# Last tile's layer norm read from PSUM, an early GpSimd broadcast, and step lists in another order, in a two-layer hybrid encoder

## The chip, the cores and the metric

The kernel runs on one core of a Trainium2 chip. A core has five engines with an instruction queue each: TensorE (PE; its weight loads are shown as PEld), VectorE (DVE), ScalarE (ACT), GpSimd (POOL) and SyncE (SP), which here only issues DMAs. The metric is the device time of one execution in microseconds (us); several executions are timed and the median counts.

## The reference

The input x has 256 tokens of 1024 values. Two layers of three sublayers each follow, every one closed by a layer norm over the residual (ALPHA is the fourth root of 4):

```
x <- LN(ALPHA*x + 0.5*SwiGLU_1(x))
x <- LN(ALPHA*x + Mixer(x))      layer 0: bidirectional chunkwise mLSTM, layer 1: windowed attention
x <- LN(ALPHA*x + 0.5*SwiGLU_2(x))

swiglu(x)    = (silu(x @ w_g) * (x @ w_u)) @ w_out        hidden width 2816
LN(x)        = (x - mean) * rsqrt(var + 1e-5) * g + b     over the 1024 values of a token
mLSTM        4 heads; input and forget gates per direction; log-forget sums along the tokens,
             running maxima, weights exp(...), then (q k^T * weights) @ v, divided by a normaliser,
             a norm per head, times sigmoid(o), @ w_out
attention    16 query heads on 4 key/value heads, |t-s| <= 128, a linear distance bias, a sink
             logit per head, softmax, @ v, @ w_out
```

All data are float32, and so is the output.

## The kernel before, in words

**Products.** Every float32 operand is split in two reduced-precision parts: ACT casts the high part (`w_hi`, `xT_hi`, `h_hi`), DVE subtracts it from the original to get the low part (`w_lo`, ...). `mm3` (line 691) makes one product of three matmuls, hi x hi, hi x lo and lo x hi. So each 128x1024 word of weights costs a DMA, one ACT cast and one DVE subtraction before PE can use it.

**Stages.** The 256 tokens are two tiles of 128. Six stages run one after the other: ffn, mlstm, ffn, ffn, attn, ffn. In an ffn, most of the up projection goes through Strassen-Winograd blocks of 512 gate and 512 up columns: `strassen` (line 907) returns seven products named P1, P2, S1, S2, S3, S4 and A22, each in two halves, one word of weights each. Some words are sums of two blocks of weights: either DVE adds two loaded words, or a DMA of POOL's queue adds the second block onto the first in SBUF (`bring`, line 926). The mLSTM's value projection is one such block as well; there A22's words are completed by a `bring` in `fourth_word`.

**The order on PE is written by hand.** The strings at lines 47 to 57 name the steps of PE in order, with a count behind `*`. In the blocks of an ffn (FIRST, FULL, SHUT, OPEN): `d` is one chunk of the down projection (12 matmuls of 512 columns), `T0` and `T1` turn a block's hidden values of token tile 0 and 1 (four transposes into a PSUM bank, then a high and a low part by ACT and DVE), `a` and `b` are the side columns, `x1` to `x4` the sums of x that Strassen's products need, `p` what is left of the stage before. OPEN is the first block of a stage with five blocks, FIRST the first of the stage with four (the run's first), SHUT the last of a stage, FULL those between. `T1` turns the values of the block before; in them the product `e<-g,e` is made after A22. In MIXES (mLSTM): `u` is a unit of the output gate, `q` a unit of the query and key projection (three matmuls of 256 columns), `g` the gate projection with the scans behind it, `c` four small transposes that turn the scans' results into columns, `H0` to `H3` the score products of a head, `M0` to `M3` its mixing with the values, `sig` a sigmoid. In HEADS (attention): `P`, `S`, `E`, `N`, `T`, `V` are a head pair's score products, masked scores, exponentials, scaling, transposes and value products, `y0` and `y1` units of the output projection.

**The order on the other engines is planned.** `Book` (line 253) notes each step without running it. `cost` gives each a length, `latest` a due time (counted back from the PE step that needs it), and `sequence` walks through a simulated time: of the steps that could start first on an engine, the one with the earliest due time goes next. The same walk gives each tile its buffer and each result its PSUM bank; the bank that is free first is taken, and one that PE hasn't fully written goes ahead of a written one. `emit` (line 591) then issues every step, so that all instructions carry line 600 in the profile. On the chip each engine runs its queue in this order and waits where an input is late. For a plain transfer in POOL's queue the plan takes the landing from `FEW` (line 63); one such transfer is `most`, another the small loads (`few`).

**The mLSTM's scans** (line 1249) start when ACT has copied the gates' forget half from PSUM to `gl`. A chain of DVE and ACT steps follows; two small transfers of POOL's queue bring four rows of the result to partitions 0, 32, 64 and 96 of `most`, and `weights(h)` (line 1290) spreads one of these rows over all partitions for each head and direction with `partition_broadcast` on POOL; ACT takes exponentials, and POOL masks them (`affine_select`).

**The layer norm** is the class `Norm` (line 761). "Seeded" means that ACT writes ca*x into the output's PSUM bank before the matmuls, which then add onto it. In most cases ACT copies the finished half to x with its sum, squares it, and DVE applies the mean with the gain, then the scale with the bias. The power -1/2 is one instruction on POOL (`tensor_tensor` with `OP.pow`). In the last stage the second token tile is "parted": it isn't seeded; DVE adds ca*x and the PSUM result into SBUF and takes statistics there. `tail` (line 827) orders the last chunks. In the last stage it does the first three chunks of the second half of columns, then all chunks of the first half, and then the last three chunks of the second half in two quarters of 256 columns, each in a bank of its own, so that only a quarter's work stands behind the last matmul.

Of the kernel before, what the change touches and what calls it, by code (L numbers as in the profile page):

```python
# [15 lines left out]
OP = mybir.AluOpType  # L16
# [34 lines left out]
OWN = [(5, 0), (6, 0), (7, 0)]  # L51
MIXES = ('P1*2 u*4 P2*2 u*2 p u*2 x1 u*4 x3 g x2 u*4 x4 S1*2 S2*2 S4*2 S3*2 q*7 A22*2 q*1 c q*29 '
         'q*1 H0 q*2 H1 q*8 M0 q*16 sig u*2 H2 M1 u*1 H3 u*3 M2 u*2 M3 u*8')
FIRST = "P1*2 d T1 P2*2 S1*2 S2*2 d S3*2 S4*2 d A22*2 T0"
FULL = "P1*2 d T1 P2*2 S1*2 S2*2 d S3*2 S4*2 d A22*2 T0 d"
SHUT = "P1*2 d T1 P2*2 S1*2 S2*2 d*2 S3*2 S4*2 A22*2 T0"
OPEN = "a*1 P1*2 a*3 p P2*2 x1 b*1 x2 S1 b*1 S1 x3 x4 b*1 S2*2 b*1 S4*2 t S3*2 d A22*2 T0"
# [5 lines left out]
FEW = {"most": 6600.0, "few": 9500.0}  # L63
# [189 lines left out]
class Book:  # L253
# [79 lines left out]
    def cost(self, s):  # L333
# [3 lines left out]
        if s.engine == "PE":  # L337
# [5 lines left out]
            if narrow != self.narrow:  # L343
                s.takes, self.narrow = s.takes + (195.0 if narrow else 146.0), narrow
# [259 lines left out]
def trunk_kernel(ctx: ExitStack, tc: tile.TileContext, x, ffn_w_in, ffn_w_out, ln_g, ln_b, ml_w_in, ml_gate_b,  # L604
# [156 lines left out]
    class Norm:  # L761
        def __init__(self, t, ca, eps, last=False, seeded=True):
            self.t, self.ca, self.eps, self.last = t, ca, eps, last
            self.parted = last and t
            self.seeded = seeded and not self.parted
            if self.parted:
                self.stats = few[:, 171:189].rearrange("p (h s) -> p h s", h=3)
            else:
                self.sums = small("sums", [128, 6])
# [4 lines left out]
        def half(self, h, y):  # L774
            z = xt[self.t][:, h * 512:(h + 1) * 512]
            if self.seeded:
                nc.scalar.activation(z, y, AF.Copy, accum_out=self.sums[:, h:h + 1])
            elif self.parted:
                nc.vector.scalar_tensor_tensor(z, z, self.ca, y, op0=OP.mult, op1=OP.add)
                nc.vector.bn_stats(self.stats[:, h], z)  # L780
            else:
                nc.vector.scalar_tensor_tensor(z, z, self.ca, y, op0=OP.mult, op1=OP.add, accum_out=self.sums[:, h:h + 1])

        def first(self, h, y):
            z = xt[self.t][:, h * 512:(h + 1) * 512]
            nc.vector.scalar_tensor_tensor(z, z, self.ca, y, op0=OP.mult, op1=OP.add)

        def quarter(self, h, q, y):
            z = xt[self.t][:, h * 512 + q * 256:h * 512 + (q + 1) * 256]
            nc.vector.tensor_add(z, z, y)  # L790
            nc.vector.bn_stats(self.stats[:, h + q], z)

        def finish(self):
# [16 lines left out]
            for s_ in cuts:  # L810
                nc.vector.scalar_tensor_tensor(z[:, s_], z[:, s_], mean, self.gain[0][:, s_],
                                               op0=off, op1=OP.mult)
# [14 lines left out]
    def tail(y, h, todo, norm, last, turn_at, between=None):  # L827
# [16 lines left out]
        for j, (o, n) in enumerate(order):  # L844
# [5 lines left out]
            if last and j == half - 1:  # L850
                norm[1].first(1, y[1][1])
            if n == full - 1:
                norm[1].half(o, y[1][o])
        if last:
            for q in range(2):
                yq = bank((128, 256))
                for n in range(half, full):
                    c, get = todo[1][n]
                    mm3(yq, h(c, 1), pair(get(), A, 0, slice(512 + 256 * q, 768 + 256 * q)), n == half, n == full - 1)
                norm[1].quarter(1, q, yq)  # L860
# [328 lines left out]
    def mlstm(l, n, pending, last):  # L1189
# [59 lines left out]
        def scans():  # L1249
            nc.scalar.copy(gl, pg[64:128])  # L1250
            nc.vector.scalar_tensor_tensor(fa[r], pg[f_], gbias[f_], gl[f_], op0=OP.add, op1=OP.add)
# [379 lines left out]
```

## Time and profile before

| | |
|---|---|
| median of 3 runs (range) | 905.94 us (904.21 to 906.06) |
| the profiled execution's own time | 904.78 us |
| its span in the trace | 903.0 us |
| busy: PE, DVE, ACT, POOL | 99%, 91%, 73%, 19% |
| mean granted clock of TensorE | 0.998 |
| DMA | 244 GB/s mean, 220.07 MB |

A line of the profile shows start and length in us, engine, line, operation, output<-inputs by the program's names, shape, and in brackets how long the engine had been idle and which instruction ended that. Groups show a count, busy time and mean length in ns. Lengths of neighbouring instructions on one engine overlap a little, on PE by almost half, so spacing is read from starts. "Waits" lists who waited for whom: total, times, longest.

### The profile page before, as it was taken

To read this page: it belongs to the slowest core of one execution; us is meant where nothing else is said; L and a number is where in the kernel's file an instruction comes from. 1 tells how busy PE (TensorE), PEld (TensorE's weight loads), DVE (VectorE), ACT (ScalarE), POOL (GpSimd) and SP (SyncE) were. 2 spreads that over 40 slices of the span, in tenths; PEclk is the share of its full clock that TensorE was granted. 3 is DMA by queue.
4 is the path that set the end of the run, shared out by engine and by line. 5 is a ranking of instruction groups with operands and counts; after the bars stand their busy time and mean duration, and the time that the engine had idled before them with its cause. 6 is when DMAs were issued, how large, how long until landed. Compare 5 with 4: busy or idle time off the path is not lost.

```text
span 903.0 us, 12647 instructions
## 1 busy us (share of the span) xinstructions
PE 890.6 (99%) x4375; PEld 741.9 (82%) x4375; DVE 824.9 (91%) x1011; ACT 655.8 (73%) x923; POOL 168.4 (19%) x200
## 2 busy tenths in 40 slices
PE   9999999999999999999999999999999999999996
PEld 7888888888888888888888888888898788888785
DVE  7999998699997999999889999996889999999974
ACT  7777676687876887776669766776789888677651
POOL 0121221220521221112021211130133231211100
PEclk9999999999999999999999999999999999999999
DMA  9999998927486989999975999999542688999931
GB/s 318 378 306 271 275 314 266 293 78 230 161 299 175 229 243 324 292 265 279 362 192 164 241 296 314 290 251 374 166 125 95 181 191 230 319 274 267 291 85 46
DMA packets 107744, 220.07 MB, mean 244 GB/s; under 512 B 7288, under 2 KB 23696, under 8 KB 107680
## 3 DMA queue, kind: packets, MB, share of 16 engines
q1 hardware_dynamic: 84000, 174.09, 54.2%
q0 software_dynamic: 23680, 45.18, 29.0%
q8 instruction: 34, 0.56, 0.2%
q14 instruction: 30, 0.25, 0.1%
HBM read 218.18 MB, written 1.05 MB: 243 GB/s over the span
## 4 chain that ended last, share of the span: by engine, by line
PE 72%; DVE 15%; issue 6%; DMA 4%; ACT 2%; POOL 1%; DVEq 0%; POOLq 0%; ACTq 0%
PE pw L600 44%; PE py L600 28%; DVE w_lo L600 8%; DMA b<-in_ffn_w_in_dram 3%; DVE b L600 1%; ACT sc L600 1%; DVE e L600 1%; DMA raw<-in_ffn_w_in_dram 1%; DVE S L600 1%; DVE scan L600 1%; DVE x L600 1%; DVE pr L600 1%; DVE pv L600 0%; DVE xT_lo L600 0%; DVE sc L600 0%
## 5 line engine op out<-in xcount | busy, mean ns | idle before, releaser
L600 ACT CAST w_hi<-b 128x1024 fp32r<-128x1024 f32 x280 | 292.0, 1053 | 103.1 <-PE py L600 50.6
L600 DVE TENSOR_TENSOR w_lo<-b,w_hi 128x1024 fp32r<-128x1024 f32 x280 | 334.0, 1217 | 9.5 <-ACT w_hi L600 9.1
L600 PE MATMUL pw<-w_hi,S 128*128 128x512 f32 x640 | 205.7, 390 | 0.0
L600 POOL DMA_DIRECT2D b<-in_ffn_w_in_dram x80 | 97.1, 1217 | 501.0 <-DVE b L600 172.6
L600 DVE TENSOR_TENSOR w_lo<-raw,w_hi 128x1024 fp32r<-128x1024 f32 (+1 forms) x150 | 178.6, 1207 | 11.4 <-ACT w_hi L600 10.5
L600 ACT CAST w_hi<-raw 128x1024 fp32r<-128x1024 f32 (+1 forms) x150 | 155.1, 1041 | 37.1 <-PE pw L600 15.9
L600 PE MATMUL pw<-w_hi,xT_hi 128*128 128x512 f32 (+1 forms) x400 | 156.6, 393 | 1.4 <-DVE h_lo L600 0.8
L600 PE MATMUL pw<-w_hi,xT_lo 128*128 128x512 f32 (+1 forms) x400 | 154.5, 388 | 0.2 <-DVE xT_lo L600 0.2
L600 PE MATMUL pw<-w_lo,xT_hi 128*128 128x512 f32 (+1 forms) x400 | 153.3, 386 | 0.0
L600 PEld LDWEIGHTS pw<-w_hi,S 128*128 128x128 f32 x640 | 120.1, 188 | 26.1 <-DVE h_lo L600 1.1
L600 PE MATMUL py<-w_hi,h_hi 128*128 128x512 f32 x317 | 125.5, 396 | 0.0
L600 PE MATMUL pw<-w_lo,S 128*128 128x512 f32 x320 | 124.5, 389 | 0.0
L600 PE MATMUL py<-w_hi,h_lo 128*128 128x512 f32 x317 | 123.7, 390 | 0.0
L600 PE MATMUL py<-w_lo,h_hi 128*128 128x512 f32 x317 | 123.4, 389 | 0.0
L600 DVE TENSOR_TENSOR b<-b,b 128x1024 f32<-128x1024 f32 x74 | 90.1, 1218 | 0.9
L600 PEld LDWEIGHTS pw<-w_hi,xT_lo 128*128 128x128 f32 x400 | 75.1, 188 | 17.5 <-DVE xT_lo L600 2.2
L600 PEld LDWEIGHTS pw<-w_hi,xT_hi 128*128 128x128 f32 x400 | 75.0, 188 | 17.0 <-DVE h_lo L600 1.6
L600 PEld LDWEIGHTS pw<-w_lo,xT_hi 128*128 128x128 f32 x400 | 75.1, 188 | 13.9
L600 PEld LDWEIGHTS pw<-w_lo,S 128*128 128x128 f32 x320 | 60.1, 188 | 12.3
L600 PEld LDWEIGHTS py<-w_hi,h_lo 128*128 128x128 f32 x317 | 59.5, 188 | 12.7
L600 PEld LDWEIGHTS py<-w_lo,h_hi 128*128 128x128 f32 x317 | 59.6, 188 | 11.8
L600 PEld LDWEIGHTS py<-w_hi,h_hi 128*128 128x128 f32 x317 | 59.5, 188 | 11.6
(208 smaller groups left out, 1130.1 us busy)
## 6 DMA issues: line engine op xcount, KB each, us to landing
b<-in_ffn_w_in_dram SPq DMA_DIRECT2D x152, 512.0 KB, 8.1
raw<-in_ffn_w_out_dram SPq DMA_DIRECT2D x88, 512.0 KB, 8.3
b<-in_ffn_w_in_dram POOLq DMA_DIRECT2D x80, 512.0 KB, 9.0
raw<-in_ffn_w_in_dram SPq DMA_DIRECT2D x36, 256.0 KB, 7.0
raw<-in_ml_w_in_dram SPq DMA_DIRECT2D x16, 512.0 KB, 6.3
raw<-in_at_w_in_dram SPq DMA_DIRECT2D x12, 512.0 KB, 9.1
b<-in_ml_w_in_dram SPq DMA_DIRECT2D x8, 512.0 KB, 6.3
raw<-in_ml_w_out_dram SPq DMA_DIRECT2D x8, 512.0 KB, 3.5
```

Source lines behind the costliest of these rows:

```text
L600: getattr(engines[s.engine], s.name)(*[real(x) for x in s.args], **{k: real(x) for k, x in s.kw.items()})
```

## The change

1. `Norm`: the parted tile is seeded like the others, its statistics are taken by `bn_stats` straight from PSUM, and the first product of `finish` reads the PSUM pieces (kept in `held`) and writes x in SBUF. The DVE adds of `half`, `first` and `quarter` are gone.
2. `tail`: after the first three chunks of the second half, ACT copies the bank in two pieces of 256 columns into two new banks, and the quarters' matmuls add onto these copies instead of starting from zero.
3. `scans`: one `partition_broadcast` of a row of `gl` into `most` right after the copy of `gl`. Its result is overwritten by the two transfers.
4. The lists HEADS, MIXES, FIRST, FULL, SHUT and OPEN are in another order.
5. The plan's costs: the landing of `most` is 8500 ns instead of 6600, and a matmul that switches between 64 and 128 rows of the array costs 255 and 230 ns more instead of 195 and 146.

```diff
 HEADS = (...
-         'q*1 S5 T31 E5 y0*1 q*5 T40 V3 y0*1 P6 S6 E6 N6 T41 y0*1 N5 y0*1 V4 T50 P7 T51 S7 E7 y0*2 '
-         'N7 V5 y1*1 T60 T61 y0*2 y1*1 V6 T70 y1*1 T71 y1*2 V7 y0*1 y1*1 y0*3')
+         'S5 T31 y0*1 q*1 E5 q*5 T40 V3 y0*1 P6 S6 E6 N6 T41 y0*1 N5 y0*1 V4 T50 P7 T51 S7 E7 y0*2 '
+         'N7 V5 y1*1 T60 T61 y0*2 V6 y1*1 T70 y1*1 T71 y1*2 V7 y0*1 y1*1 y0*3')
...
-MIXES = ('P1*2 u*4 P2*2 u*2 p u*2 x1 u*4 x3 g x2 u*4 x4 S1*2 S2*2 S4*2 S3*2 q*7 A22*2 q*1 c q*29 '
-         'q*1 H0 q*2 H1 q*8 M0 q*16 sig u*2 H2 M1 u*1 H3 u*3 M2 u*2 M3 u*8')
-FIRST = "P1*2 d T1 P2*2 S1*2 S2*2 d S3*2 S4*2 d A22*2 T0"
-FULL = "P1*2 d T1 P2*2 S1*2 S2*2 d S3*2 S4*2 d A22*2 T0 d"
-SHUT = "P1*2 d T1 P2*2 S1*2 S2*2 d*2 S3*2 S4*2 A22*2 T0"
-OPEN = "a*1 P1*2 a*3 p P2*2 x1 b*1 x2 S1 b*1 S1 x3 x4 b*1 S2*2 b*1 S4*2 t S3*2 d A22*2 T0"
+MIXES = ('P1*2 u*4 P2*2 u*2 p u*2 x1 u*4 x3 g x2 u*4 x4 S1*2 S2*2 S4*2 S3*2 q*8 c q*5 A22*2 q*25 H0 '
+         'q*2 H1 q*8 M0 q*16 M1 sig u*2 H2 u*1 H3 u*3 M2 u*2 M3 u*8')
+FIRST = "T1 P1*2 d P2*2 S1*2 S2*2 S4 d*2 S3*2 S4 A22*2 T0"
+FULL = "P1*2 d T1 P2*2 S1*2 S2*2 d S3*2 S4*2 d A22*2 d T0"
+SHUT = "T1 P1*2 d P2*2 S1*2 S2*2 d*2 S3*2 S4*2 A22*2 T0"
+OPEN = "a*1 P1*2 a*3 p P2*2 x1 b*1 x2 S1 b*1 S1 S2 x3 x4 b*1 S2 b*1 S4*2 t S3*2 d A22*2 T0"
...
-FEW = {"most": 6600.0, "few": 9500.0}
+FEW = {"most": 8500.0, "few": 9500.0}
...
             if narrow != self.narrow:
-                s.takes, self.narrow = s.takes + (195.0 if narrow else 146.0), narrow
+                s.takes, self.narrow = s.takes + (255.0 if narrow else 230.0), narrow
...
             self.parted = last and t
-            self.seeded = seeded and not self.parted
+            self.seeded = seeded
+            self.held = []
...
         def half(self, h, y):
             z = xt[self.t][:, h * 512:(h + 1) * 512]
-            if self.seeded:
+            if self.parted:
+                nc.vector.bn_stats(self.stats[:, h], y)
+                self.held.append((slice(h * 512, h * 512 + 512), y))
+            elif self.seeded:
                 nc.scalar.activation(z, y, AF.Copy, accum_out=self.sums[:, h:h + 1])
-            elif self.parted:
-                nc.vector.scalar_tensor_tensor(z, z, self.ca, y, op0=OP.mult, op1=OP.add)
-                nc.vector.bn_stats(self.stats[:, h], z)
             else:
...
-        def first(self, h, y):
-            z = xt[self.t][:, h * 512:(h + 1) * 512]
-            nc.vector.scalar_tensor_tensor(z, z, self.ca, y, op0=OP.mult, op1=OP.add)
-
         def quarter(self, h, q, y):
-            z = xt[self.t][:, h * 512 + q * 256:h * 512 + (q + 1) * 256]
-            nc.vector.tensor_add(z, z, y)
-            nc.vector.bn_stats(self.stats[:, h + q], z)
+            nc.vector.bn_stats(self.stats[:, h + q], y)
+            self.held.append((slice(h * 512 + q * 256, h * 512 + q * 256 + 256), y))
...
             cuts = [slice(0, 512), slice(512, D)] if self.last else [A]
-            for s_ in cuts:
-                nc.vector.scalar_tensor_tensor(z[:, s_], z[:, s_], mean, self.gain[0][:, s_],
+            for s_, v in self.held or [(s_, z[:, s_]) for s_ in cuts]:
+                nc.vector.scalar_tensor_tensor(z[:, s_], v, mean, self.gain[0][:, s_],
                                                op0=off, op1=OP.mult)
...
             if last and j == half - 1:
-                norm[1].first(1, y[1][1])
+                yq = [bank((128, 256)) for _ in range(2)]
+                for q in range(2):
+                    nc.scalar.copy(yq[q], y[1][1][:, 256 * q:256 * q + 256])
...
             for q in range(2):
-                yq = bank((128, 256))
                 for n in range(half, full):
                     c, get = todo[1][n]
-                    mm3(yq, h(c, 1), pair(get(), A, 0, slice(512 + 256 * q, 768 + 256 * q)), n == half, n == full - 1)
-                norm[1].quarter(1, q, yq)
+                    mm3(yq[q], h(c, 1), pair(get(), A, 0, slice(512 + 256 * q, 768 + 256 * q)), False, n == full - 1, True)
+                norm[1].quarter(1, q, yq[q])
...
         def scans():
             nc.scalar.copy(gl, pg[64:128])
+            nc.gpsimd.partition_broadcast(most[:, 0], gl[0:1])
```

## The prediction

> **What bounds the kernel now.** I read the page first, then PE's waits over the whole run, then the order of time on PE, DVE and POOL at the places the change touches.
>
> ```profile
> span 903.0 us, 12647 instructions
> PE 890.6 (99%) x4375; PEld 741.9 (82%) x4375; DVE 824.9 (91%) x1011; ACT 655.8 (73%) x923; POOL 168.4 (19%) x200
> ...
> L600 ACT CAST w_hi<-b 128x1024 fp32r<-128x1024 f32 x280 | 292.0, 1053 | 103.1 <-PE py L600 50.6
> ```
>
> TensorE works for 99% of the span, and DVE, which subtracts out every low half after ACT has cast the high one, is close behind at 91%. The change removes no matmul, so it can win only what PE waits, and what stands behind the last matmul.
>
> ```profile
> PE pw L600 <- DVE h_lo L600: 0.8, 1, 0.8
> PE py L600 <- DVE a_lo L600: 0.7, 1, 0.7
> PE pw L600 <- DVE k_lo L600: 0.4, 2, 0.2
> ...
> PE py L600 <- DVE q_lo L600: 0.3, 1, 0.3
> ```
>
> These are the largest of PE's waits behind the start-up; none reaches a microsecond. The a_lo wait opens the mixing of the mLSTM's first head:
>
> ```profile
> 237.47 0.39 PE L600 MATMUL py<-v_hi,a_hi 128*128 128x258 f32 x1 [0.16 <-ACT a_hi L600]
> 237.69 0.28 PE L600 MATMUL py<-v_lo,a_hi 128*128 128x258 f32 x1
> 238.63 0.39 PE L600 MATMUL py<-v_hi,a_lo 128*128 128x258 f32 x1 [0.66 <-DVE a_lo L600]
> ```
>
> Printed waits leave out part of a gap, so I take it from the starts: 0.94 where 0.12 is usual (21 such matmuls, the seven q units, fill 214.39 to 216.91 in the rows below). With the 0.16 ahead of it that is 1.0 us. The h_lo wait is at a seam between two Strassen blocks of the last stage:
>
> ```profile
> 846.16 0.60 PE L600 MATMUL pw<-ident,e 128*128 128x128 f32 x4
> ...
> 849.14 0.39 PE L600 MATMUL py<-w_hi,h_lo 128*128 128x512 f32 x1
> 850.30 0.50 PE L600 MATMUL pw<-w_hi,xT_hi 128*128 128x512 f32 x1 [0.77 <-DVE h_lo L600]
> ```
>
> There are 1.16 us between two starts, against 0.23 (216.91 to 217.14 below): 0.9 us. P1 of the new block takes the bank that T0's transposes filled at 846.16, and it is free only when DVE has read it, behind another product:
>
> ```profile
> 848.96 0.68 DVE L600 TENSOR_TENSOR e<-g,e 128x512 f32<-128x512 f32 x1
> 849.56 0.68 DVE L600 TENSOR_TENSOR h_lo<-pw,h_hi 128x512 fp32r<-128x512 f32 x1
> ```
>
> **The change part by part.**
>
> *The early broadcast.* POOL in the mLSTM, the landing of the `most` transfers, the durations of the broadcasts, the input of the next power, and ACT's copy of the keys:
>
> ```profile
> 201.88 1.20 POOL L600 DMA_DIRECT2D b<-in_ml_w_in_dram  x1 [0.53 <-DVE w_lo L600]
> 219.62 1.21 POOL L600 DMA_DIRECT2D most<-scan  x2 [16.55 <-ACT w_hi L600]
> 227.59 4.21 POOL L600 PARTITION_BROADCAST wt<-most  x4 [6.76 <-ACT v_hi L600]
> ...
> 249.29 0.81 POOL L600 TENSOR_TENSOR hrs<-hrs,few 128x2 f32<-128x2 f32 x1 [6.91 <-DVE k_lo L600]
> ...
> DMA to landing us min/median/max: 1.7/1.7/1.7
> ...
> L600 POOL PARTITION_BROADCAST wt<-most x8: 547/548/2967, 227.6 to 241.8; - x8
> ...
> 246.36 0.17 DVE L600 TENSOR_SCALAR hrs<-hmv 128x2 f32<-128x2 f32 x1
> ...
> 230.90 0.58 ACT L600 ACTIVATE k_hi<-pw 128x512 fp32r<-128x512 f32 x1
> ```
>
> Both `most` transfers have been issued by 220.83 and land 1.7 after their issue, by about 222; the first broadcast starts at 227.59 and takes 2.97, where others take 0.55. The power at 249.29 likewise starts 2.8 after its input (246.36+0.17). Both gaps are 6.8 to 6.9 us, and both stand where POOL turns from one kind of work to the other. I read them as a fixed cost of that turn; the engines named as releasers (v_hi, k_lo) make nothing that these two instructions read. A broadcast right behind the copy of gl pays the turn between 201 and 211, in the 16.55 us in which POOL idles. Until the real broadcasts only DMAs follow; if these leave the turn paid (no row here tells; it is a rival below), the real ones begin about 227.59-222 = 5 us earlier, and the first of them is 2.4 shorter. The weights' exponentials, a_hi and a_lo hang on them: the 1.0 us at head 0 goes, at best also the 0.4 of k_lo, whose copy on ACT (row 230.90) stands among the exponentials. Bounds: nothing, since ACT and DVE keep their written order and the plan now believes the landing 1.9 us later (8500 for 6600), and -1.4. I take -1.4, because c moves forward past the two words of A22, 12 matmuls of 0.23 = 2.7 us: the scans and `most` are due earlier by more than the 1.9.
>
> *What it is moved past.* The second `b` transfer (row 201.88) completes the sum that A22 multiplies by. The w_lo that releases it and the copy of gl:
>
> ```profile
> 200.12 1.22 DVE L600 TENSOR_TENSOR w_lo<-b,w_hi 128x1024 fp32r<-128x1024 f32 x1
> ...
> 200.97 0.37 ACT L600 COPY gl<-pw 64x256 f32<-64x256 f32 x1 [0.62 <-PE pw L600]
> ...
> DMA to landing us min/median/max: 6.7/7.7/8.7
> ...
> 214.39 0.28 PE L600 MATMUL pw<-xT_hi,w_hi 128*128 128x256 f32 x1
> ...
> 216.91 0.40 PE L600 MATMUL pw<-w_hi,xT_hi 128*128 128x512 f32 x1
> 217.14 0.40 PE L600 MATMUL pw<-w_lo,xT_hi 128*128 128x512 f32 x1
> ```
>
> Both end at 201.34, so either can come first in POOL's queue. With the broadcast first, the transfer and the `most` pair queue behind it: the transfer starts at 201.34+6.76+2.97 = 211.1 instead of 201.88, lands 6.7 to 8.7 later (the landings of the two `b` transfers here; 217.8 to 219.8), and its cast (1.05) and subtraction (1.22) end at 220.1 to 222.1. PE, which had A22 at 216.91, now has it behind 13 units q of 0.36 and c (about 0.4, four small transposes), and reaches its second word 6 matmuls further: 214.39+4.7+0.4+1.4 = 220.9. So A22 is 0 to 1.2 late; with the transfer first nothing is. I take +0.4. The word's buffer comes free later by as much, and SP's next load into it; those are weights of the output projection, a stage end away.
>
> *The lists.* In FULL, T0 goes behind its d. Then T0's bank is not yet read when P1 starts, and the planner, which takes the bank that is free first, has those of the finished products. That removes the h_lo wait: 0 to -0.9; I take -0.9. SHUT and FIRST now begin with T1, which needs e<-g,e. It ended at 849.64; PE would come to T1 behind d and T0 at 846.16+2.8+0.4 = 849.4. Five such places (a FIRST and four SHUTs) of 0 to 0.3 each; DVE gets that product with an earlier due time, so I take +0.2 in all. In HEADS, T31 and V6 go ahead of one unit each; the q_lo wait belongs to the last head's output, which is not moved: 0 to -0.3, I take -0.1. S2's earlier half in OPEN and the planner's dearer switch of array height (255 and 230 for 195 and 146) only reorder work that lies under a busy PE: 0, and where that cover is gone one w_lo, 1.2, either way.
>
> *The tail.* DVE behind the last matmul, that matmul, and three groups that price the new forms:
>
> ```profile
> 895.34 0.43 DVE L600 BATCH_NORM_STATS2 few<-x 128x6 f32<-128x256 f32 x1
> 895.72 0.42 DVE L600 TENSOR_TENSOR x<-x,pw 128x256 f32<-128x256 f32 x1
> 896.17 0.43 DVE L600 BATCH_NORM_STATS2 few<-x 128x6 f32<-128x256 f32 x1
> 896.64 0.23 DVE L600 BATCH_NORM_AGGREGATE mv<-few 128x2 f32<-128x18 f32 x1
> ...
> 896.98 1.40 DVE L600 SCALAR_TENSOR_TENSOR x<-x,mv,ln_g 128x512 f32<-128x512 f32 x2
> 898.30 1.40 DVE L600 SCALAR_TENSOR_TENSOR x<-x,rs,ln_b 128x512 f32<-128x512 f32 x2
> ...
> 895.40 0.28 PE L600 MATMUL pw<-w_hi,h_lo 128*128 128x256 f32 x1
> ...
> L600 DVE SCALAR_TENSOR_TENSOR h<-py,den,h 128x256 f32<-128x256 f32 x8 | 3.5, 473 | 0.0
> L600 DVE TENSOR_TENSOR e<-pw,e 128x512 f32<-128x512 f32 x20 | 13.6, 682 | 0.1
> L600 DVE TENSOR_TENSOR e<-e,e 128x512 f32<-128x512 f32 x19 | 13.1, 691 | 0.6
> ```
>
> The last quarter's add goes (896.17-895.72 = 0.45): the statistics can start when the last matmul ends, 895.68, as the add did. The earlier adds go too, off this path. The product with the gain becomes 512+256+256 wide: 0.66 (half of 898.30-896.98) plus twice about 0.41 (473 ns less the overlap of 0.06 that the 256-wide add and statistics show) against 1.32, so +0.16. Net -0.3; bounds -0.45 and -0.1. Statistics read from PSUM have no row here; the two groups of e show that a PSUM operand costs nothing over SBUF (682 against 691). [...] The two copies of 256 columns cost ACT at most 0.37 each by the copy of gl, the two more seeds of 512 at most twice that, and ACT, 73% busy, does them under PE's work; without that cover they are 0.7 and 1.5.
>
> Sum: -1.4+0.4-0.9+0.2-0.1-0.3 = -2.1. On the profiled execution's 904.78 (span 903.0 and 1.8 around it) that is 902.7; on the median of the runs shown, 905.94, it is 903.8. The waits that go are of the kind that a later landing lengthens, so I put the forecast between the two: **903.3**.
>
> **The rivals.**
>
> *The waits come back elsewhere.* With PE at 99% and DVE at 91%, a PE that no longer waits at one place meets the next late subtraction. For it speaks that all PE waits on one DVE, whose total work stays. Against it: away from the quoted rows, PE's waits are smaller still, so DVE keeps up nearly everywhere. Left are the tail and half of head 0: -0.3-0.5 = -0.8, 904.0 to 905.1.
>
> *Slower: the transfer behind the broadcast.* If it lands at 219.8, its cast holds up ACT and its subtraction DVE, and four subtractions for the next q words stand behind:
>
> ```profile
> 220.12 4.62 DVE L600 TENSOR_TENSOR w_lo<-raw,w_hi 128x1024 fp32r<-128x1024 f32 x4
> ```
>
> 1.2 for A22 and up to 4.6 for these make 5.8, less 2.5 gained elsewhere: +3.3, 908.1 to 909.2. It decides from a landing after 220.9-1.05-1.22 = 218.6. Against it: the planner may well run those subtractions first. [...]
>
> *It doesn't do what it says.* The turn is paid again before the real broadcasts: head 0 stays as it is, and the sum is -2.1+1.4 = -0.7, 904.1 to 905.2.
>
> *All of it and more.* No new wait, and the reordered work 1.2 on the good side: -1.4-0.9-0.3-0.45-1.2 = -4.3, 900.5 to 901.6.
>
> **How the numbers follow.** About 0.2%, 1.8 us, is what a measurement here can tell from no change: faster is below 904.1, slower above 907.8. Forecast 0.50 (its own range 901.7 to 904.8), waits come back 0.25, slower 0.15, not done 0.05, all and more 0.05. Faster takes 0.43 of the forecast's chance and the last case's 0.05: 0.48. Slower is its rival's 0.15 and 0.02 of the forecast's for edits under cover that isn't there: 0.17. The same has the rest, 0.35. The range, 901.0 to 907.5, reaches over the waits that come back and leaves out the slow rival.
>
> **What would show it.** Right: a long first broadcast near 208 and no gap of 6.8 us before the real ones, heads mixed without an a_lo wait, no h_lo wait at a seam, the last statistics starting with the end of the last matmul. Wrong: a second such gap; a PE wait on w_lo near 221; PE waiting at a block's start for T1's input; an ACT queue that holds the exponentials back although the broadcasts are early.

## The result, and the profile after

The changed kernel takes 910.29 us (909.27 to 910.77) against 905.91 (904.21 to 906.06) before: a ratio of 1.0053, 95% interval 1.0038 to 1.0068. It is slower by about 4.8 us, where 2.6 us less than before were forecast. The profiled execution took 910.77 us. From the profile's page:

```profile
span 909.1 us, 12673 instructions
...
PE 892.3 (98%) x4375; PEld 743.6 (82%) x4375; DVE 823.9 (91%) x1008; ACT 656.5 (72%) x927; POOL 169.8 (19%) x201
```

The span grew by 6.1 us; the work of DVE and ACT is what it was. To find the place I compared when the n-th matmul starts in both traces. At the first matmul of the mLSTM the new kernel is 0.1 us ahead, at the last one of it 6.3 behind, and at the last of all 6.4 behind. The other five stages come out level together, so the loss is in the mLSTM. Below, the length of a stage is always read in this way, by the starts of its first and its last matmul. That is finer than the span of one execution: e8 below, whose first stage isn't changed, is 1.2 us behind after the first 40 us. PE's waits in the mLSTM (and one, on `e`, in the last stage):

```profile
PE py L600 <- ACT a_hi L600: 2.0, 1, 2.0
...
PE pw L600 <- ACT w_hi L600: 1.2, 2, 0.7
PE pw L600 <- DVE k_lo L600: 0.8, 1, 0.8
PE pw L600 <- DVE w_lo L600: 0.8, 1, 0.8
PE pw L600 <- DVE e L600: 0.6, 1, 0.6
```

Before, no wait behind the start-up reached a microsecond, and the one for a_hi was 0.2. There are two places. The first is A22. POOL in order of time, and then the view of the tile `b`, which says how long the transfer of 211.13 took to land:

```profile
200.05 1.21 POOL L600 DMA_DIRECT2D b<-in_ml_w_in_dram  x1 [8.74 <-DVE w_lo L600]
209.48 1.80 POOL L600 PARTITION_BROADCAST most<-gl  x1 [8.22 <-DVE w_lo L600]
211.13 1.43 POOL L600 DMA_DIRECT2D b<-in_ml_w_in_dram  x1
217.04 1.22 POOL L600 DMA_DIRECT2D most<-scan  x2 [4.48 <-issue]
221.28 0.54 POOL L600 PARTITION_BROADCAST wt<-most  x1 [3.02 <-DMA most<-scan]
224.52 2.81 POOL L600 PARTITION_BROADCAST wt<-most  x2 [2.70 <-DVE w_lo L600]
...
247.26 0.96 POOL L600 PARTITION_BROADCAST wt<-most  x2 [1.24 <-issue]
255.50 0.73 POOL L600 TENSOR_TENSOR hrs<-hrs,few 128x2 f32<-128x2 f32 x1 [7.27 <-issue]
```

```profile
DMA to landing us min/median/max: 9.8/9.8/9.8
```

The planner put the broadcast between the two `b` transfers. The turn does move to the front (8.22 us of idle ahead of `most<-gl`), and the first real broadcast, at 221.28, has no such gap, takes 0.54 and starts 6.3 us earlier than before. But the second transfer goes out at 211.13 instead of 201.88 and lands at 221. What waits for it on ACT and then on PE:

```profile
220.99 1.05 ACT L600 CAST w_hi<-b 128x1024 fp32r<-128x1024 f32 x1 [8.51 <-DMA b<-in_ml_w_in_dram]
...
229.99 0.62 ACT L600 CAST v_hi<-e 128x512 fp32r<-128x512 f32 x1 [1.55 <-DVE e L600]
...
231.46 1.57 ACT L600 ACTIVATE wt<-wt,ucol 128x128 f32<-128x128 f32 x5
```

```profile
220.97 0.39 PE L600 MATMUL pw<-w_hi,xT_lo 128*128 128x512 f32 x1
222.09 0.50 PE L600 MATMUL pw<-w_hi,xT_hi 128*128 128x512 f32 x1 [0.74 <-ACT w_hi L600]
223.35 0.50 PE L600 MATMUL pw<-w_lo,xT_hi 128*128 128x512 f32 x1 [0.76 <-DVE w_lo L600]
```

ACT stands still for 8.5 us with its later steps behind that cast, and PE loses 0.9 + 1.0 us (1.12 and 1.26 between starts where 0.23 is usual). DVE waits as well, and what stands behind is late:

```profile
222.07 1.23 DVE L600 TENSOR_TENSOR w_lo<-b,w_hi 128x1024 fp32r<-128x1024 f32 x1 [2.64 <-ACT w_hi L600]
223.22 5.05 DVE L600 TENSOR_TENSOR w_lo<-raw,w_hi 128x1024 fp32r<-128x1024 f32 x4
...
229.07 0.28 DVE L600 COPY ucol<-pw 128x128 f32<-128x128 f32 x1
```

The exponentials of head 0 read the broadcast rows, the first of them there since 221.8, and `ucol`, which DVE copies behind A22's subtraction and the four for q, at 229.07. In ACT's queue they stand behind the cast of 229.99, which waits for `e`, DVE's next product. So they start at 231.46 (before: 230.59): the broadcasts are early and the exponentials are not. DVE makes k_lo at 234.09 (before: 231.51), behind its late subtractions; that is the k_lo wait, 1.04 between two starts on PE.

The second place is the third head's mixing, M2. DVE and PE:

```profile
256.27 0.50 DVE L600 TENSOR_SCALAR h<-h,hmv,hrs 128x256 f32<-128x256 f32 x1 [2.83 <-POOL hrs L600]
256.69 1.00 DVE L600 TENSOR_TENSOR wt<-pw,wt 128x512 f32<-128x512 f32 x2
```

```profile
256.20 0.39 PE L600 MATMUL pw<-w_hi,xT_lo 128*128 128x512 f32 x1
258.62 0.39 PE L600 MATMUL py<-v_hi,a_hi 128*128 128x258 f32 x1 [2.03 <-ACT a_hi L600]
...
259.61 0.39 PE L600 MATMUL py<-v_hi,a_lo 128*128 128x258 f32 x1 [0.49 <-DVE a_lo L600]
...
262.73 0.63 PE L600 MATMUL pw<-w_lo,xT_hi 128*128 128x512 f32 x1
263.15 0.63 PE L600 MATMUL pw<-w_hi,xT_lo 128*128 128x512 f32 x1
```

Head 0's scaling (`h<-h,hmv,hrs`) needs the power on POOL, and POOL pays its second turn ahead of that: 7.27 us from the last broadcast at 248.22 to 255.50. In DVE's queue the scaling now stands ahead of the product of scores and weights (`wt<-pw,wt`) from which a_hi is cast, so DVE idles for 2.83 us, and PE has 2.4 us between two starts (256.20 to 258.62) and then 0.8 (258.84 to 259.61). Then a second cost comes: the matmuls of 512 columns that follow start 0.42 us apart instead of 0.23. Two stretches of that time, with TensorE's granted clock as the number behind POOL's busy time:

```profile
256.00:259.00 3.00, 0.97 (x5) 0.46 (x3) 2.55 (x6) 1.27 (x3) 1.03 (x3) 1.00 1.00 350
...
261.00:262.00 1.00, 1.00 (x6) 1.00 (x6) 1.00 (x3) 0.58 (x3) 0.00 (x0) 0.50 0.43 142
```

The row's 0.50 is the clock. By the spacing of the starts it is halved from 260.8 to 264.0, after PE has worked again for two microseconds, and takes another 1.6 us.

Less the usual spacing these are 1.9 us at A22, 0.9 at k_lo, 2.8 at M2 and 1.6 for the clock. Without the 1.0 that head 0's a_lo wait took before, that makes 6.2 of the 6.4.

### The profile page after: what moved, and what is told of

Read it like the earlier page. It is cut to its first block, busy times and chain, and to the rows that moved or that the text cites. A ratio compares the mean times of both kernels' runs of the same rounds, so it can differ in the third digit from the quotient of the medians.

```text
span 909.1 us, 12673 instructions
## 1 busy us (share of the span) xinstructions
PE 892.3 (98%) x4375; PEld 743.6 (82%) x4375; DVE 823.9 (91%) x1008; ACT 656.5 (72%) x927; POOL 169.8 (19%) x201
## 4 chain that ended last, share of the span: by engine, by line
PE 73%; issue 10%; DVE 8%; DMA 4%; ACT 3%; POOL 2%; DVEq 0%; SPq 0%; POOLq 0%; ACTq 0%
PE pw L600 45%; PE py L600 28%; DVE w_lo L600 3%; DMA b<-in_ffn_w_in_dram 2%; ACT w_hi L600 1%; POOL b L600 1%; DMA b<-in_ml_w_in_dram 1%; DMA raw<-in_ffn_w_in_dram 1%; DVE e L600 0%; DVE pv L600 0%; DMA raw<-in_ffn_w_out_dram 0%; DVE x L600 0%; DVE h L600 0%; ACT sc L600 0%; POOL rs L600 0%
```

## The experiments

My theory after these views: the loss is the broadcast ahead of the transfer, plus the new MIXES at M2; the block lists and the tail gain what was forecast. The runs are called e1 to e16 in the order in which they come. The rival is that one cause explains both places: everything in the mLSTM is late because A22 is late.

**The broadcast, out and in.** First (e1) the changed kernel without its early broadcast:

```diff
             nc.scalar.copy(gl, pg[64:128])
-            nc.gpsimd.partition_broadcast(most[:, 0], gl[0:1])
```

> The changed kernel without the early broadcast, all else as changed. Queue theory (the broadcast and its turn of POOL hold back the transfer that completes A22's words, ACT then stands on that word's cast, and the whole mLSTM is late): the transfer is issued near 202 again, ACT's idle of 8.5 us before the cast is gone, PE's waits in the mLSTM fall from about 8.4 to 3 us, and the time is 904 to 905.5, 5 to 6 below the changed kernel. List theory (c, A22 and M1 in their new places and the landing of 8500 make the loss by themselves): 908 to 910, as changed.

Measured: 906.33 us, 1.0024 of before (1.0014 to 1.0034), a little above the range of the first theory. The w_hi and w_lo waits are gone and ACT no longer stands still; M2 still waits (a_hi, 1.6). By the ratios the broadcast costs the changed kernel 0.0029, 2.6 us; the profiled spans (909.1 and 903.6) are 5.5 apart, but the one is of the longest of five executions and the other of the shortest of eleven. In the mLSTM the two differ by 5.2 us. And a second cause is left that has nothing to do with A22: the rival falls.

Then (e2) the kernel before with only that broadcast added:

```diff
             nc.scalar.copy(gl, pg[64:128])
+            nc.gpsimd.partition_broadcast(most[:, 0], gl[0:1])
```

> The kernel before with the early broadcast alone. Queue theory: the same 9 us on the transfer, with A22 2.9 us earlier on PE than in the changed kernel, so PE waits 4 to 5 us at A22's second word: 909 to 913. List theory: about as before, 904 to 906, or 1 less for the earlier weights of head 0.

Measured: 911.81 us, 1.0083 (1.0070 to 1.0096). PE in order of time, and the stretch behind it:

```profile
217.97 0.39 PE L600 MATMUL pw<-w_hi,xT_lo 128*128 128x512 f32 x1
222.12 0.80 PE L600 MATMUL pw<-w_hi,xT_hi 128*128 128x512 f32 x1 [3.76 <-ACT w_hi L600]
223.38 0.80 PE L600 MATMUL pw<-w_lo,xT_hi 128*128 128x512 f32 x1 [0.46 <-DVE w_lo L600]
```

```profile
223.00:232.00 9.00, 8.56 (x35) 7.57 (x36) 8.32 (x11) 5.29 (x8) 4.93 (x4) 0.52 0.19 59
```

In the order of before, A22 comes six units q and c earlier on PE, 2.9 us, so the starts lie 4.1 us apart instead of 1.1, and then PE runs for about 9 us at half its clock (0.52 in the row). The changed order takes the edge off the broadcast.

**The broadcast behind the transfer.** The turn was to be paid early without a transfer queued behind it, in the changed kernel (e3) and in the one before (e4):

```diff
-            nc.gpsimd.partition_broadcast(most[:, 0], gl[0:1])
...
             nc.vector.tensor_scalar(fm[r], fa[r], 0.0, None, op0=OP.min)
+            nc.gpsimd.partition_broadcast(most[:, 0], fm[0:1])
```

> The changed kernel with its broadcast taken from a later step of the scans (row fm instead of gl), so that it stands behind the transfer in POOL's queue and ahead of the most transfers. Queue theory: transfer near 202, turn paid in POOL's idle time, no gap before the real broadcasts: 902.5 to 904.5, and below the changed kernel without a broadcast by up to 1.4. List theory: 908 to 910.

> The kernel before with that later broadcast alone. Prices the turn by itself: if the 6.8 us gap before the real broadcasts carries PE's 1.0 at head 0 and the 0.4 of k_lo, the time is 1.0 to 1.4 below before (904.5); if ACT's and DVE's written order holds the weights back anyway, it is within 0.5 of before.

Measured: 907.98 us, 1.0043 (1.0029 to 1.0057), and 905.26 us, 1.0002 (0.9991 to 1.0014). Neither gains, and the first lies far above its forecast. But the row `fm` is written again by a later step of the scans, which had to wait until the broadcast had read it, so these two mix the turn with late scans (PE waits 0.5 for `scan` in the first). They don't settle what the turn alone is worth.

**MIXES, out and in.** The changed kernel without the broadcast and with the MIXES of before (e5); and the kernel before with the new MIXES, its costs unchanged (e6). The first edit, of which the second is the reverse without the broadcast:

```diff
-            nc.gpsimd.partition_broadcast(most[:, 0], gl[0:1])
...
-  ... S3*2 q*8 c q*5 A22*2 q*25 H0 q*2 H1 q*8 M0 q*16 M1 sig u*2 H2 u*1 H3 ...
+  ... S3*2 q*7 A22*2 q*1 c q*29 q*1 H0 q*2 H1 q*8 M0 q*16 sig u*2 H2 M1 u*1 H3 ...
```

> The changed kernel without the early broadcast and with the old list MIXES; the landing of most stays at 8500 in the plan. In the run without a broadcast PE waits 2.4 us at the third head's mixing: DVE stands 2.8 us at head 0's scaling, whose power is behind POOL's second turn (6.9 us), and head 2's weights are queued behind it. Mixes theory (M1's new place brings the power and head 2's weights into this order): the wait goes, 903.5 to 905, 1.5 to 2.5 below the run without a broadcast. Plan theory (the landing of 8500 does it): the wait stays, 906 to 907.

> The kernel before with the new MIXES alone. Mixes theory: the 2.4 us at the third head's mixing appear, 1.0 us at head 0 may go: 906 to 907.5. Plan theory: no such wait, 904 to 905.

Measured: 903.62 us, 0.9976 (0.9964 to 0.9988), with no wait at M2; and 919.18 us, 1.0150 (1.0128 to 1.0173), far above both theories. In the second, POOL shows why:

```profile
251.04 0.73 POOL L600 TENSOR_TENSOR hrs<-hrs,few 128x2 f32<-128x2 f32 x1 [7.48 <-issue]
260.67 0.98 POOL L600 PARTITION_BROADCAST wt<-most  x2 [8.90 <-issue]
...
270.50 0.73 POOL L600 TENSOR_TENSOR hrs<-hrs,few 128x2 f32<-128x2 f32 x1 [6.91 <-DVE w_lo L600]
```

The plan put head 0's power ahead of the last broadcasts: three turns in place of one, and PE waits 13.3 us for a_hi. In the changed kernel the last broadcasts stay ahead of the power. The dearer landing of `most` (8500) may be what keeps them there; no run changes it alone. The plan itself knows no turn.

**The parts that were to gain.** The kernel before with FIRST, FULL, SHUT and OPEN alone (e7), of which the seam's edit is shown; and with the last tile's norm alone (e8; points 1 and 2 of the change, as in its diff):

```diff
-FULL = "P1*2 d T1 P2*2 S1*2 S2*2 d S3*2 S4*2 d A22*2 T0 d"
+FULL = "P1*2 d T1 P2*2 S1*2 S2*2 d S3*2 S4*2 d A22*2 d T0"
```

> The kernel before with the new FIRST, FULL, SHUT and OPEN alone. As forecast: the h_lo waits at seams go (0.9 to 1.3 at the last stage), T1 at a block's start waits for its product 0 to 0.7 in single places: -0.7 against before, 904.0. Rival: the waits only change places, within 0.4 of before.

> The kernel before with the new layer norm of the last tile alone. As forecast -0.3: from the last matmul's start to the end of the span 7.3 instead of 7.6. [...]

Measured: 903.97 us, 0.9982 (0.9971 to 0.9993), and 905.11 us, 0.9991 (0.9977 to 1.0004). In the first the eight transposes of the seam run without a break (PE):

```profile
848.34 1.03 PE L600 MATMUL pw<-ident,e 128*128 128x128 f32 x8
```

In the second, 7.3 us lie between the start of the last matmul and the end of the span, against 7.6 (903.0 - 895.40) before.

**What remains without MIXES, HEADS and broadcast, and a clean late broadcast.** The run e5 with the HEADS of before as well (e9); that kernel with a broadcast from `ig`, a row that is complete behind the second transfer and not written again soon (e10); the kernel before with the same (e11); and the changed kernel with the MIXES of before, its broadcast kept (e12):

```diff
                 nc.vector.scalar_tensor_tensor(ig[32 * d:32 * d + 32], pg[r], gbias[r], gl[r], ...)
+            nc.gpsimd.partition_broadcast(most[:, 0], ig[0:1])
```

> The changed kernel without the early broadcast and with the mLSTM's order MIXES and the last-but-one stage's order HEADS of before: what stays of the change is the block lists, the planner's two costs (broadcasts and narrow switches) and the last tile's norm. Theory (the whole loss sits in the broadcast and in the new MIXES; blocks gain 1.6 us and the tail 0.3 to 0.8): 903.0 to 904.0 us, 0.9970 to 0.9985 of before, no product waiting for the exponentials' or the power's result longer than before. If HEADS carries a gain of its own (0.1 us was forecast), the kernel that keeps it, 0.9976, stays level or better than this one. Rival (the gain of the run with new HEADS came from HEADS): this one falls back to 0.9990 or above.

> The same kernel with the early broadcast put behind the second transfer of b and ahead of the issue of most, reading a row of the gates' sum that is complete there and is not overwritten soon (the input gates with their bias). POOL's turn (some 7 us) is then paid while DVE computes the scans, and no transfer and no step of the scans is queued behind it. Theory (the turn alone is worth something only where PE waits for the weights of head 0): against the kernel without it the product that waits at the start of head 0 and the k_lo wait shrink, 0 to 1.0 us gained, 902.3 to 904. Rival (ACT and DVE take their steps in written order, so that earlier broadcasts change nothing): no difference above 0.3 us, and head 0's exponentials start within 0.5 us of where they started without it. The issue of most now stands behind the broadcast: if the broadcast ends after the scans, most starts late and it costs up to 1 us.

> The kernel before with that late broadcast from the input gates alone, to give the price of the turn by itself without what the earlier late run mixed in (there a step of the scans waited for the broadcast to read its row). Theory: the order of before keeps its waits; 904.9 to 905.9 us, 0.9988 to 1.0 of before, with the gap at head 0 (0.8 us) gone and half or more of it back at the h_lo seam or at k_lo. Rival (the forecast's term of 1.4 us was right and only its place was wrong): 904.3 to 904.6 us, 0.9983 to 0.9987, the gaps gone for good.

> The changed kernel with the mLSTM's order of before: the broadcast stays ahead of the second transfer of b. In the order of before the two casts of A22 stand ahead of c, so what the late transfer holds back on ACT and DVE is the cast of A22 and all that is written behind it. Theory (the price of the broadcast is the delay of that transfer, and the new MIXES, which puts A22 behind c, takes part of it): PE waits 3 to 4 us for w_hi at the second half of A22, as in the kernel before with the broadcast alone, and the time is 908 to 911 us, so that new MIXES gains 0 to 2 us with the broadcast where it loses 2.7 us without. Rival (the two losses simply add): 906.2 us, the run without both plus the 2.6 us that the broadcast costs under the new order.

Measured, in this order: 904.88 us, 0.9990 (0.9981 to 0.9998); 905.43, 0.9993 (0.9984 to 1.0001); 904.92, 0.9991 (0.9982 to 1.0000); 912.19, 1.0074 (1.0059 to 1.0089).

e9 came out 0.0014 above e5, against my expectation. By its waits it pays 0.7 for `sc` in the attention and 0.6 for `e` at a seam, which e5 doesn't. The old HEADS with the new costs and blocks is then about 1 us worse than the new one; the two intervals overlap a little, so this is likely and no more.

e11 is the clean price of the turn. In the trace the exponentials of head 0 start at 228.98 instead of 230.59, and the mLSTM is 1.1 us shorter than before. But the rest of the run gives it back: the last matmul starts when it did before (0.1 us later), and most of the return is in the last stage, where the h_lo seam now takes 1.55 us between two starts (848.82 to 850.37) instead of 1.16. POOL and PE of e11:

```profile
221.65 4.75 POOL L600 PARTITION_BROADCAST wt<-most  x4 [0.65 <-DMA most<-scan]
...
850.37 0.50 PE L600 MATMUL pw<-w_hi,xT_hi 128*128 128x512 f32 x1 [1.16 <-DVE h_lo L600]
```

The time is 0.9 us shorter by the ratio, with an interval that reaches 1. e4 shows the same: the mLSTM 1.2 us shorter, the last stage 1.2 longer. This is the prediction's first rival, waits that come back elsewhere. In e10, on top of e9, nothing is left of the gain (0.9993 against 0.9990), as its rival had it.

e12 against the changed kernel, 1.0074 to 1.0053, shows that the new MIXES gains 2 us under the broadcast, while without it (e1 against e5, 1.0024 to 0.9976) it loses 4: the two edits don't add.

**Which move of MIXES.** New MIXES makes two moves: c goes ahead of A22, and M1 goes ahead of `sig u*2 H2`. Three kernels (e13 to e15) take them apart, and a fourth (e16) asks again after the turn:

```diff
-  ... q*8 c q*5 A22*2 q*25 H0 q*2 H1 q*8 M0 q*16 M1 sig u*2 H2 u*1 H3 ...
+  ... q*8 c q*5 A22*2 q*25 H0 q*2 H1 q*8 M0 q*16 sig u*2 H2 M1 u*1 H3 ...
```

The first has only this edit; the second also has no broadcast; the third has no broadcast, A22 ahead of c as before, and M1 early; the fourth is the second with the broadcast from `ig`.

> The changed kernel, early broadcast and all, with one word of MIXES moved back: M1 stands again behind sig u*2 H2, so that PE has H2 and two units o before it. Theory (the 2.7 us that the new MIXES costs come from this move: DVE gets head 0's scaling, which waits for POOL's second turn, ahead of the score products of the head that PE mixes next): the 2.0 us wait for a_hi is gone, DVE no longer idles over 2 us ahead of h<-h,hmv,hrs, and the time is 907.3 to 908.3 us, 1.0018 to 1.0028 of before, what the broadcast costs under this order remaining. Rival (the loss comes from the first half of the list, where c and A22 changed places, since the scores' exponentials are then in another order on POOL and ACT): the wait stays, 909.5 to 910.8.

> The same without the early broadcast: c stays ahead of A22 and M1 goes back. Theory (M1): 903.3 to 904.3 us, level with the run that had the whole list of before (0.9976), and no wait for a_hi over 0.3 us. Rival (first half): 905.8 to 906.6, as with the new list (1.0024).

> The counterpart: A22 ahead of c as before, M1 early as in the change, no early broadcast. Theory (M1): the wait for a_hi of 1.5 to 2.5 us stays and the time is 905.5 to 907.5 us. In this kernel's queue the last broadcasts are spread over two places, still ahead of the power, so that there is one turn only. Rival (first half): no such wait, 903.3 to 904.3.

> As the run without the broadcast and with M1 back, with the broadcast from the input gates behind the second transfer of b: the turn is paid early, the transfer is not held up, and c stands early, so that the scans and most are due early. If the turn was worth the forecast's 1.4 us anywhere, it is here: 902.0 to 903.0 us. Theory (ACT's and DVE's written order and not the turn sets when head 0 is ready): within 0.6 us of the run without it.

Measured: 907.03 us, 1.0018 (1.0008 to 1.0029); 902.18, 0.9967 (0.9955 to 0.9980); 908.60, 1.0034 (1.0021 to 1.0047); 904.96, 0.9993 (0.9980 to 1.0006). It is M1. With it back there is no wait for a_hi. With it early PE waits at the mixing of a later head whatever stands in the first half; in e15 it is 4.1 us for the fourth head's a_lo, more than was expected, and again DVE has it behind the scaling, for which it idles 4.67 us. DVE in e14, at the place where it idled:

```profile
248.04 1.01 DVE L600 TENSOR_TENSOR wt<-pw,wt 128x512 f32<-128x512 f32 x2
248.97 0.81 DVE L600 TENSOR_SCALAR h<-h,hmv,hrs 128x256 f32<-128x256 f32 x2
```

The scores' product is ahead of the scaling, and by then the power (247.73) is done. Four of the kernels make a square:

| ratio to before | M1 early (as changed) | M1 as before |
|---|---|---|
| with the early broadcast | 1.0053, span 909.1, mLSTM +6.4 | 1.0018, span 905.3, mLSTM +2.3 |
| without it | 1.0024, span 903.6, mLSTM +1.2 | 0.9967, span 900.2, mLSTM -1.2 |

By the ratios either edit costs 0.5% to 0.6% on top of the fast corner, and both together 0.9%; by the spans 5.1 us (broadcast) and 3.4 (M1), and 8.9 together. Within what the times can tell these two add. The mLSTM by itself is finer: the broadcast costs 3.5 us with M1 back and 5.2 with M1 early, M1 costs 2.4 and 4.1. Together they cost 1.7 us more than one by one. That is about what the half clock takes in the changed kernel (1.6); e1's shorter stall at M2 left the clock at 1.00. The rest of the difference between the spans is in the last stage, where e14 gains 1.2 us on before and the other three nothing. What clearly doesn't add is the other move: c ahead of A22 is worth 0.0056 with the broadcast (e12 to e13) and 0.0009, no more than the uncertainty, without it (e5 to e14). It gives the late transfer time. The corner without both edits, e14, is the best kernel of the study: 902.18 us, faster than before by 3.0 us (1.8 to 4.1).

e16 is slower than e14 although its turn is paid early. In order of time, DVE and ACT of e14, then POOL, DVE and ACT of e16:

```profile
220.25 4.62 DVE L600 TENSOR_TENSOR w_lo<-raw,w_hi 128x1024 fp32r<-128x1024 f32 x4
...
226.30 0.62 ACT L600 CAST v_hi<-e 128x512 fp32r<-128x512 f32 x1 [1.67 <-DVE e L600]
...
227.77 1.57 ACT L600 ACTIVATE wt<-wt,ucol 128x128 f32<-128x128 f32 x5
```

```profile
220.13 0.97 POOL L600 PARTITION_BROADCAST wt<-most  x1 [1.63 <-DMA most<-scan]
...
220.60 5.27 DVE L600 TENSOR_TENSOR w_lo<-raw,w_hi 128x1024 fp32r<-128x1024 f32 x4
...
222.12 2.81 POOL L600 PARTITION_BROADCAST wt<-most  x2 [1.03 <-DVE w_lo L600]
...
227.30 0.62 ACT L600 CAST v_hi<-e 128x512 fp32r<-128x512 f32 x1 [2.40 <-DVE e L600]
...
228.78 1.56 ACT L600 ACTIVATE wt<-wt,ucol 128x128 f32<-128x128 f32 x5
```

In both, ACT takes the exponentials right behind a cast of v_hi that waits for DVE, not for POOL. In e16 the broadcasts now run beside DVE's four subtractions, which start 0.35 us later and take 5.27 us instead of 4.62, and the exponentials come 1.0 us later with them.

## Why the prediction was wrong

Two steps made the loss. A third, the gain of the block lists, came out in other kernels and not in this one.

*"What it is moved past"* is the first. It had the mechanism right: the planner does put the broadcast first, and the transfer starts at 211.13. That this is the 211.1 of the forecast is in part luck: the turn took 8.2 us where 6.76 was taken, and the broadcast 1.8 where 2.97 was. It had the landing at 6.7 to 8.7 us from the transfers of before, and it was 9.8: at 221, past the 218.6 from which the slower rival was to decide. That rival's chain is what happened: cast, then subtraction, then the four subtractions for q behind it. Taken were +0.4; the runs give 2.6 us with M1 early and 4.6 with M1 back by the ratios (0.0029 and 0.0051), and 5.2 and 3.5 in the mLSTM of the traces. These readings don't agree well; 2.6 to 5 us is what can be said. The rival's 5.8 for this chain was close to the upper end; 15% for it was too little, since two landings are no bound for a third. "The planner may well run those subtractions first" was the wrong comfort: the order on ACT and DVE is fixed by planned landings, and the plan thinks of a broadcast as a step of about 1 us.

*"The lists"* is the second. It went through HEADS, FIRST, FULL, SHUT and OPEN, and took from MIXES only that c moves ahead. That M1 moves ahead of `sig u*2 H2` has no price there at all. It costs 0.0035 with the broadcast and 0.0057 without (3 and 5 us; 4.1 and 2.4 in the mLSTM of the traces). The row for it was quoted: the power at 249.29 starts 2.8 us after its input, behind the second turn. The sum asked what the first turn delays and not who stands behind the second: DVE's scaling of head 0, and behind it in DVE's queue the weights of the next head on PE. No rival had it either.

*"The early broadcast", -1.4.* Right in size for the one stage, and credited to the wrong edit. The turn alone is worth 1.1 us in the mLSTM where nothing is queued behind it (e11), and there the later stages give it back. But the a_lo wait of head 0 also goes without any early broadcast, and without moving c: in e5 and e9, which have the MIXES of before, it is gone and the mLSTM is 0.9 us shorter, though the turn is paid at the old place (5.64 and 5.78 us of idle ahead of the first broadcast). The blocks alone (e7) and the tail alone (e8) leave that wait as it was, so the plan's two costs are what is left as the reason; no run changes them alone, and this stays open. With c ahead as well (e14) it is 1.2 us. With the turn paid early on top there is nothing more to gain (e16, e10): that ACT's and DVE's written order could hold the weights back stood as the lower bound of this step, and that bound was the answer. Nor was the first broadcast's 2.97 part of the turn, as the step had it: in e11 the first of the four at 221.65 takes 3.52 with the turn long paid.

*The seam, -0.9, T1 +0.2, HEADS -0.1.* Alone, the blocks are worth 0.0018, 1.6 us, where -0.7 was taken: in e7's trace the h_lo wait is gone, with 1.2 in the last stage and the rest before it. In the changed kernel h_lo no longer waits either, but the last stage is no shorter than before. T1 waits at the same seam, and for longer than the 0.3 allowed (the changed kernel in order of time); smaller waits ahead of it take the rest:

```profile
855.98 0.68 DVE L600 TENSOR_TENSOR e<-g,e 128x512 f32<-128x512 f32 x1
...
856.73 0.65 PE L600 MATMUL pw<-ident,e 128*128 128x128 f32 x4 [0.56 <-DVE e L600]
```

e1, e9, e10 and e13 have this wait too; e3, e5, e7, e12 and e14 to e16 don't, and their last stage is 1.1 to 1.2 us shorter than before. So whether `e<-g,e` comes in time hangs on the plan as a whole, and what decides it stays open. The attention with the new HEADS is 0.15 to 0.3 us longer than before in these traces, not 0.1 shorter; HEADS was not run by itself.

*The tail, -0.3.* Right: 7.3 us behind the start of the last matmul (901.75) instead of 7.6, and 7.3 with the tail alone; the time, 0.9991 (0.9977 to 1.0004), can't tell it from nothing. DVE at the end:

```profile
902.07 0.43 DVE L600 BATCH_NORM_STATS2 few<-pw 128x6 f32<-128x256 f32 x1 [0.65 <-PE pw L600]
...
902.88 0.74 DVE L600 SCALAR_TENSOR_TENSOR x<-py,mv,ln_g 128x512 f32<-128x512 f32 x1
```

The statistics read from PSUM take the 0.43 that they took from SBUF, and the first product takes 0.74 from PSUM as it did from SBUF (742 ns each before).

Without the price of the transfer the sum was -1.4-0.9+0.2-0.1-0.3 = -2.5. The kernel without the two edits, e14, gives -3.0 by the ratio and -2.8 by its span: -1.20 in the mLSTM, -1.17 in the last stage, -0.33 behind the last matmul, +0.25 in the attention and -0.38 in the other stages. That the total fits is partly luck, since the first of these didn't need the edit it was credited to. In the changed kernel the mLSTM lost 6.4 and the last stage gained nothing. What decided was what waits behind a moved instruction in its queue.

## What to carry to other kernels

When a slow instruction is moved to where its engine idles, look at what that engine issues next, DMAs above all, and price the latest landing by more than the rows at hand (9.8 us here, where the rows had 6.7 and 8.7): an engine that waits for it holds everything behind it, as ACT did for 8.5 us. Go through every word of a changed list; one that wasn't priced cost about as much as the one that was argued about. An order made for one edit can be worth 5 us with it and nothing without: time edits of one stage in a square. And where a planner orders the rest, compare stage by stage: an edit in one stage changed another by 1 us.

## What the hardware showed that was not expected

*The turn has its mark in the trace.* POOL's queue shows two instructions at each turn of the two kernels (200.8 and 248.1 in the changed one). In the kernel before, by line and operation, ahead of the first broadcast and ahead of the first power:

```profile
L600 POOLq MODIFY_POOL_CONFIG  x2: 37/37/37, 220.8 to 220.9; - x2
...
L600 POOLq MODIFY_POOL_CONFIG  x2: 127/127/127, 242.3 to 242.3; - x2
```

The next work of POOL starts 6.7 and 7.0 us after these; in the runs quoted here the engine idles for 5.6 (e5) to 8.9 us (e6) at a turn, and longer where a broadcast of the scans' rows also had to wait for its row (10.0 in e16). It is paid in both directions, between broadcasts and the power: in e6 7.48 us ahead of the power at 251.04, 8.90 ahead of the broadcast at 260.67. `affine_select` runs between broadcasts without one (before, 232.20 to 241.42, where POOL never idles over 1.24), and the DMAs that POOL issues in the changed kernel at 211.13 and 217.04 don't bring it back: the broadcast at 221.28 follows 3.02 us of idle that the landing of `most` ended. A transfer queued behind the turn waits (211.13 instead of 201.88). What POOL does in a turn no run shows.

*A stall of PE was paid twice.* After 4.1 and 1.3 us between two starts (e2) TensorE ran about 9 us at a granted clock of one half (0.52), after 2.4 and 0.8 (changed kernel) 3.2 us, after 2.0 and 0.8 (e1, 252.17 to 255.17) or 1.1 and 1.3 (A22 in the changed kernel, 1.00 from 223 to 232) not at all. At half the clock the matmuls of 512 columns start 0.42 us apart (rows 262.73 and 263.15), and in the changed kernel the clock fell 2.2 us after PE had started again (258.62 to 260.8). What decides whether it falls no run shows.

*Broadcasts and DVE's subtractions took longer side by side.* A broadcast takes 0.54 us with DVE idle (221.28 in the changed kernel), 1.46 and 1.49 beside subtractions of whole words (224.52), and up to 4.08 (e5, 227.39). Before, the first one, of 2.97, ends 0.4 us behind the last of three such subtractions that were already running. Those three take 3.48 us, as they do with no broadcast beside them (e14, 226.78), so there only the broadcast takes longer. At other places DVE's work does: four subtractions take 4.62 us by themselves (before, 220.12) and 5.05 to 5.27 beside broadcasts (the changed kernel, 223.22; e16, 220.60). The start of the next broadcast (230.43 before) bears the 2.97 out.
